# The order of a recurrence's score products on TensorE: head after head, or the two heads in turn

## The chip, the cores and the metric

The kernel runs on one core of one Trainium2 chip. The metric is the device time of one execution in microseconds (us). Before the change it is 2375.42 us, the median of three runs (2374.48 to 2377.20).

## The reference, cut to what matters

The program is a stack of blocks on one sequence of 512 positions and width 1024: an attention block with a gated feed-forward part, a block with an RWKV-7 recurrence and a feed-forward part, and a third block with two linear recurrences. Only the RWKV-7 block matters here. It runs a state recurrence for 16 heads of width 64, once forwards and once backwards in time:

```python
def rwkv7_scan(r, w, k, v, kk, a):
    def step(state, inp):
        r_t, w_t, k_t, v_t, kk_t, a_t = inp
        sa = jnp.einsum('bhvk,bhk->bhv', state, -kk_t)
        state = (state * w_t[:, :, None, :] + sa[..., None] * (kk_t * a_t)[:, :, None, :]
                 + v_t[..., None] * k_t[:, :, None, :])
        return state, jnp.einsum('bhvk,bhk->bhv', state, r_t)
```

For each direction the output is group-normed, a bonus term is added, and it is gated; the two directions are summed.

## The kernel before, in words

The recurrence is computed in chunks of 64 positions, eight chunks in each direction. The 16 heads are taken as eight pairs (`p` = 0 to 7); a pair fills the 128 partitions, head 0 the lower 64 (`H(0)`) and head 1 the upper 64 (`H(1)`). Chunk `n` of the forward direction goes with chunk `7 - n` of the backward one (`chunk_of`), and the two directions are worked on together (`d` = 0, 1).

Ten streams, written as Python generators, do the work of a pair. `front` (line 1483) and the two `half` (L1520, one for each direction) prepare the decayed keys and queries: the tiles `bk` (keys, one for each direction and each half of the chunks) and `ar` (queries). `scores` (L1602) multiplies them: in four blocks of two chunks (`i` = 0 to 3), for each head `hp` four matmuls of `bk` and `ar` that contract over that head's 64 partitions and write 128x128 results into an accumulator bank of PSUM. DVE then multiplies a head's bank with the causal masks `mk` into the tile `at` (the mask product), parts of `at` go by DMA to `nd_s` in DRAM, and PE transposes the `bk` of the block (L1636), which ACT copies into `at`. `inverse` (L1643) waits until the four blocks of a pair are done and inverts the 32x32 triangles, some sixty small DVE instructions on `X` and `xt_`, then stores `X`; `merge` (L1688) reads the inverses back through DMA as `yz` and joins them to 64x64; `mid` (L1737) forms the chunk's transition `m` from them (matmuls `ident,ar`, `uv,at`, `ax,tt`, `at,ta`); `chain` (L1798) carries the state `ss` through the eight chunks in a bank `cp` (matmuls `ss,m`; ACT writes the next `ss`); `post` (L1838) norms and gates the output `o`; `early` (L1666) prepares the values `uv`.

The order of all this is made while the program is built, by `weave` (L36). Each stream yields ahead of an operation the engine and the tiles that it needs, or a condition such as "the chain has done so many steps". `weave` keeps an own reckoning of when every engine will be free and every tile ready, and always advances the stream that could start first; the order in which instructions of one engine come out is then fixed. Its price for a matmul (`cost`, L48) lets two neighbours run side by side only where they differ in columns of the array; it makes no such allowance for rows, nor for the wait for an accumulator bank to come free.

All banks named `mb` come from one pool of five (`pm`), handed out in turn; `cp` has three of its own. A bank is written again once what was read from it five grants earlier has been read. The matmul helper is `MM` (L1302), so matmuls of all streams carry that line and are told apart by their tiles: the score products are `mb<-ar,bk`, 64 rows by 128 columns (`64*128`), each of them two instructions in the trace, since the operands are 32-bit floats. A run of one head in one block is thus eight instructions (x8), and the two heads on end sixteen (x16).

Of the kernel before, what the change touches and what calls it, by code (L numbers as in the profile page):

```python
# [24 lines left out]
class Net:  # L25
# [200 lines left out]
    def bank(self):  # L226
        return self.ps.tile([128, 512], F32, name="mm", tag="mm")
# [1063 lines left out]
    def rwkv(self, g_pre, mu_p, mu_n, w_r, w_k, w_v, w_o, k_k, k_a, r_k, gn_w, gn_b, w0, w1, w2, a0, a1, a2,  # L1291
# [5 lines left out]
        V, G = nc.vector, nc.gpsimd  # L1297
        TT = lambda e, o, a, b, op: e.tensor_tensor(out=o, in0=a, in1=b, op=op)  # L1298
# [3 lines left out]
        MM = lambda o, l, r, a, b: nc.tensor.matmul(o, lhsT=l, rhs=r, start=a, stop=b)  # L1302
        M, AD, SU, BY = ALU.mult, ALU.add, ALU.subtract, ALU.bypass
# [23 lines left out]
        with ExitStack() as c0:  # L1327
# [105 lines left out]
            with ExitStack() as c1:  # L1433
# [4 lines left out]
                mk = sh.tile([128, 2, 128], F32, name="mk")  # L1438
# [13 lines left out]
                bank = lambda: pm.tile([128, 512], F32, name="mb", tag="mb")  # L1452
                T2 = lambda tag, bufs=2: tp.tile([128, 520], F32, name="tmp", tag=tag, bufs=bufs)
                TQ = lambda: T2("tmq", 3)[:, :S]
                H = lambda i: slice(64 * i, 64 * i + 64)
# [3 lines left out]
                flat = lambda t: t.rearrange("p a b -> p (a b)")  # L1459
                chunk_of = lambda n: (n, 7 - n)  # L1460
                rows = lambda p: slice(p * 128, (p + 1) * 128)

                PE, AC, DV, PO = "PE", "Activation", "DVE", "Pool"
# [138 lines left out]
                def scores(p, st):  # L1602


                    nt_ = T2("nt", 1)[:, :S].rearrange("p (a b) -> p a b", b=32)
                    for i in range(4):
                        yield lambda: min(done["side", 0], done["side", 1]) > 2 * p + i // 2 and done["step"] >= 2 * (4 * p + i - 9) + 2
                        bk, ar = ([st[x] for x in y] for y in ((("bk", 0, i // 2), ("bk", 1, i // 2)), (("ar", 0), ("ar", 1))))
                        bks = lambda d, c: flat(bk[d][:, c % 4])

                        at = qp.tile([128, 2, 2, 3, 128], F32, name="at", tag="at")
                        for hp in range(2):
                            yield PE, *bk, *ar
                            b = bank().rearrange("p (j x) -> p j x", j=2)
                            for j in range(2):
                                for d in range(2):
                                    c = chunk_of(2 * i + j)[d]
                                    MM(b[:, j, 128 * d:128 * d + 128], bks(d, c)[H(hp)], flat(ar[d][H(hp), c]), True, True)
                            yield DV, b
                            TT(V, at[:, :, hp, 0::2, :], b.rearrange("p j (d x) -> p j d x", d=2), mk.unsqueeze(1).to_broadcast([128, 2, 2, 128]), M)  # L1620
                        yield DV, at
                        for g in (2, 3, 0, 1):
                            d = g // 2
                            e = 64 * d + 32 * (g % 2)
                            s_ = at[Q(g), :, :, 2 * d, e:e + 32].rearrange("p j h t -> p (j h) t")
                            if g >= 2:
                                V.transpose(out=nt_[Q(g), 4 * i:4 * i + 4], in_=s_)
                                s_ = nt_[Q(g), 4 * i:4 * i + 4]
                            nc.sync.dma_start(out=nd_d[p, 16 * g + 4 * i:16 * g + 4 * i + 4].rearrange("x (s t) -> s x t", t=32), in_=s_)
                        done["pre"] += i == 3  # L1630
                        st["at", i] = at
                        yield PE, *bk
                        b = bank().rearrange("p (j d x) -> p j d x", j=2, d=2)
                        for j in range(2):
                            for d in range(2):
                                nc.tensor.transpose(b[:, j, d, :], bks(d, chunk_of(2 * i + j)[d]), self.ident)  # L1636
                        done["bk"] += i % 2
                        yield AC, b
                        for j in range(2):
                            ACT(at[:, j, :, 1].rearrange("p h (d x) -> p h d x", d=2), b[:, j].rearrange("p d (h x) -> p h d x", h=2), AF.Copy)  # L1640
                        st["q", i] = at
# [247 lines left out]
                def each(f):  # L1889
                    for p in range(8):  # L1890
                        yield from f(p, sts[p])

                self.weave([(each(f), 0.0) for f in (
                    chain, mid, inverse, early, merge, scores, front, lambda p, st: half(p, st, 0), lambda p, st: half(p, st, 1), post)])


# [166 lines left out]
```

## Time and profile before

| | |
|---|---|
| median of three runs | 2375.42 us |
| the profiled execution | 2374.26 us, of which the span (first to last instruction) is 2372.5 us |
| TensorE matmul (PE) | busy 2148.4 us, 91% of the span |
| VectorE (DVE) | busy 1350.9 us, 57% |
| ScalarE (ACT) | busy 1084.0 us, 46% |
| GpSimd (POOL) | busy 82.7 us, 3% |
| mean granted TensorE clock | 0.936 of full speed |
| score products, whole program | 512 instructions, 85.4 us busy, 330 ns mean |

Most of the span is dense projections in other blocks. The recurrence lies between about 865 and 1390 us of the span: the score products run from 866.1 to 1284.7 us. A row of a timeline merges neighbouring instructions of one engine with the same line and tiles; its second number reaches from the first start to the last end, and the last end of a matmul lies beyond the start of the next row, because matmuls are pipelined. How long a run holds PE is therefore read from its start to the next row's start.

### The profile page before, as it was taken

The page shows a single profiled execution, that of the slowest core. Times are in us where ns is not written, and L with a number is a line of the kernel's source. Part 1 is how long each engine was busy: PE and PEld are TensorE (multiplying, and loading weights), DVE is VectorE, ACT ScalarE, POOL GpSimd, SP SyncE. Part 2 cuts the span into 40 slices and gives each one's busy share as a digit, 9 for nine tenths or more (in the row PEclk, how much of TensorE's full clock was granted, in tenths as well). Part 3 has the DMA queues.
Part 4 walks back from the last instruction along what each step waited for, and adds up shares of the span by engine and source line. Part 5 has one row for each costly group of instructions (what it writes and reads, how often), then busy time and mean ns, then how long its engine had stood idle before and what let it go on. Part 6 is the DMA issues. An engine that isn't in the chain of part 4 may idle for free. (4 is left out here: it accounts for less than half of the span.)

```text
span 2372.5 us, 36431 instructions
## 1 busy us (share of the span) xinstructions
PE 2148.4 (91%) x14218; PEld 1737.5 (73%) x14218; DVE 1350.9 (57%) x2862; ACT 1084.0 (46%) x1958; POOL 82.7 (3%) x121
## 2 busy tenths in 40 slices
PE   8998999999978965788888779999999999999998
PEld 6777788888756854667666658888787877788877
DVE  4556542333479568487867446287655657732353
ACT  4555353342356454567665645342333444532232
POOL 0000000000000001011111000000000000000000
PEclk9999999999979985788889989999999989899999
DMA  5311233233332423233323153234244454233341
GB/s 170 102 54 53 80 107 92 86 107 97 99 103 63 146 65 74 43 65 67 75 44 72 49 173 105 89 109 124 97 134 128 143 133 115 66 90 100 104 142 54
DMA packets 352375, 226.54 MB, mean 95 GB/s; under 512 B 114799, under 2 KB 306315, under 8 KB 352203
## 3 DMA queue, kind: packets, MB, share of 16 engines
q1 hardware_dynamic: 350762, 218.97, 32.8%
q10 hardware_dynamic: 1440, 5.24, 0.6%
q8 instruction: 112, 1.84, 0.3%
q14 instruction: 61, 0.49, 0.1%
HBM read 193.94 MB, written 27.07 MB: 93 GB/s over the span
## 5 line engine op out<-in xcount | busy, mean ns | idle before, releaser
L160 ACT ACTIVATE whi<-raw 128x1024 fp32r<-128x1024 f32 x228 | 239.6, 1052 | 603.0 <-PE mm L223 318.2
L161 DVE TENSOR_TENSOR wlo<-raw,whi 128x1024 fp32r<-128x1024 f32 x228 | 276.3, 1214 | 385.8 <-ACT whi L160 383.0
L222 PE MATMUL mm<-uth,whi 128*128 128x512 f32 (+1 forms) x1088 | 411.7, 380 | 1.7 <-ACT uth L196 1.7
L223 PE MATMUL mm<-utl,whi 128*128 128x512 f32 (+1 forms) x1088 | 406.0, 374 | 5.3 <-DVE utl L197 5.3
L224 PE MATMUL mm<-uth,wlo 128*128 128x512 f32 (+1 forms) x1088 | 406.2, 374 | 0.0
L223 PEld LDWEIGHTS mm<-utl,whi 128*128 128x128 f32 x1088 | 208.1, 191 | 42.9 <-DVE utl L197 6.6
L222 PEld LDWEIGHTS mm<-uth,whi 128*128 128x128 f32 x1088 | 207.8, 192 | 40.5 <-ACT uth L196 2.9
L224 PEld LDWEIGHTS mm<-uth,wlo 128*128 128x128 f32 x1088 | 208.0, 191 | 37.1 <-issue 1.1
L224 PE MATMUL mm<-whi,hl 128*128 128x512 f32 x512 | 200.6, 394 | 0.0
L222 PE MATMUL mm<-whi,hh 128*128 128x512 f32 x512 | 200.5, 394 | 0.0
L223 PE MATMUL mm<-wlo,hh 128*128 128x512 f32 x512 | 199.9, 393 | 0.0
L224 PEld LDWEIGHTS mm<-whi,hl 128*128 128x128 f32 x512 | 96.3, 188 | 22.0 <-issue 0.2
L223 PEld LDWEIGHTS mm<-wlo,hh 128*128 128x128 f32 x512 | 96.3, 188 | 21.7
L222 PEld LDWEIGHTS mm<-whi,hh 128*128 128x128 f32 x512 | 96.3, 188 | 21.4 <-issue 0.4
L1302 PE MATMUL mb<-ar,bk 64*128 64x128 f32 x512 | 85.4, 330 | 16.1 <-DVE ar L1298 13.8
L223 PE MATMUL mm<-mx,whi 128*128 128x512 f32 x224 | 91.3, 407 | 4.5 <-DVE mx L1289 4.4
L222 PE MATMUL mm<-whi,uth 128*128 128x512 f32 x224 | 88.5, 401 | 6.7 <-ACT whi L160 6.4
L222 PE MATMUL mm<-mx,whi 128*128 128x512 f32 x224 | 87.3, 410 | 7.2 <-ACT mx L1288 6.2
L1302 PEld LDWEIGHTS mb<-ar,bk 64*128 64x128 f32 x512 | 72.6, 227 | 24.6 <-issue 15.5
L224 PE MATMUL mm<-mx,wlo 128*128 128x512 f32 x224 | 90.0, 402 | 0.0
L224 PE MATMUL mm<-whi,utl 128*128 128x512 f32 x224 | 88.5, 398 | 0.0
L223 PE MATMUL mm<-wlo,uth 128*128 128x512 f32 x224 | 88.0, 396 | 0.0
(534 smaller groups left out, 3887.9 us busy)
## 6 DMA issues: line engine op xcount, KB each, us to landing
raw<-in_mlp_w_dram SPq DMA_DIRECT2D x128, 512.0 KB, 4.1
raw<-in_w_in_dram SPq DMA_DIRECT2D x44, 512.0 KB, 3.8
raw<-in_attn_w_in_dram SPq DMA_DIRECT2D x18, 512.0 KB, 4.2
gbt<-in_norm_g_dram ACTq DMA_DIRECT2D x8, 512.0 KB
raw<-in_attn_w_out_dram SPq DMA_DIRECT2D x8, 512.0 KB
raw<-in_rk_w_k_dram SPq DMA_DIRECT2D x8, 512.0 KB, 4.4
h_s<-h SPq DMA_DIRECT2D x8, 512.0 KB, 2.7
raw<-in_rk_w_v_dram SPq DMA_DIRECT2D x8, 512.0 KB
```

Source lines behind the costliest of these rows:

```text
L160: nc.scalar.activation(out=hi[:, :n], in_=raw[:, :n], func=AF.Copy)
L161: nc.vector.tensor_tensor(out=lo[:, :n], in0=raw[:, :n], in1=hi[:, :n].bitcast(F32), op=ALU.subtract)
L222: mm(out, lhsT=lhs[0], rhs=rhs[0], start=start, stop=False)
L223: mm(out, lhsT=lhs[0], rhs=rhs[1], start=False, stop=False)
L224: mm(out, lhsT=lhs[1], rhs=rhs[0], start=False, stop=stop)
L1302: MM = lambda o, l, r, a, b: nc.tensor.matmul(o, lhsT=l, rhs=r, start=a, stop=b)
```

## The change

In each block the score products of the two heads are now issued in turn, head 0, head 1, head 0, head 1, each head into a bank of its own, and both banks are taken before the first product. The two mask products follow after all eight matmuls. Before, each head's four matmuls were a step of their own, which `weave` could separate from the other head's by work of other streams.

```diff
                         at = qp.tile([128, 2, 2, 3, 128], F32, name="at", tag="at")
+                        yield PE, *bk, *ar
+
+                        bs = [bank().rearrange("p (j x) -> p j x", j=2) for _ in range(2)]
+                        for j in range(2):
+                            for d in range(2):
+                                c = chunk_of(2 * i + j)[d]
+                                for hp in range(2):
+                                    MM(bs[hp][:, j, 128 * d:128 * d + 128], bks(d, c)[H(hp)], flat(ar[d][H(hp), c]), True, True)
                         for hp in range(2):
-                            yield PE, *bk, *ar
-                            b = bank().rearrange("p (j x) -> p j x", j=2)
-                            for j in range(2):
-                                for d in range(2):
-                                    c = chunk_of(2 * i + j)[d]
-                                    MM(b[:, j, 128 * d:128 * d + 128], bks(d, c)[H(hp)], flat(ar[d][H(hp), c]), True, True)
-                            yield DV, b
-                            TT(V, at[:, :, hp, 0::2, :], b.rearrange("p j (d x) -> p j d x", d=2), mk.unsqueeze(1).to_broadcast([128, 2, 2, 128]), M)
+                            yield DV, bs[hp]
+                            TT(V, at[:, :, hp, 0::2, :], bs[hp].rearrange("p j (d x) -> p j d x", d=2), mk.unsqueeze(1).to_broadcast([128, 2, 2, 128]), M)
                         yield DV, at
```

As the streams yield elsewhere now, `weave` writes another order on every engine of the recurrence. Three places follow. First PE, at the third block (`i` = 2) of pair 3; `mb_` and a number is one grant of a bank, and the first number behind `bk` is the direction. Before:

```order
L1302 MATMUL mb_8410<-ar0_7911,bk01_7963 128x128
L1302 MATMUL mb_8410<-ar1_7915,bk11_7965 128x128
L1302 MATMUL mb_8410<-ar0_7911,bk01_7963 128x128
L1302 MATMUL mb_8410<-ar1_7915,bk11_7965 128x128
L1302 LDWEIGHTS zb_6290
L1302 MATMUL cp_8415<-zb_6290 128x256
L1302 MATMUL cp_8415<-uv0_7055,at_6920 64x64 x4
L1302 MATMUL cp_8415<-uv1_7056,at_6920 64x64 x4
L1302 MATMUL mb_8427<-ar0_7911,bk01_7963 128x128
L1302 MATMUL mb_8427<-ar1_7915,bk11_7965 128x128
L1302 MATMUL mb_8427<-ar0_7911,bk01_7963 128x128
L1302 MATMUL mb_8427<-ar1_7915,bk11_7965 128x128
```

The same place after the change:

```order
L1302 MATMUL mb_8407<-ar0_7908,bk01_7922 128x128
L1302 MATMUL mb_8408<-ar0_7908,bk01_7922 128x128
L1302 MATMUL mb_8407<-ar1_7916,bk11_7931 128x128
L1302 MATMUL mb_8408<-ar1_7916,bk11_7931 128x128
L1302 MATMUL mb_8407<-ar0_7908,bk01_7922 128x128
L1302 MATMUL mb_8408<-ar0_7908,bk01_7922 128x128
L1302 MATMUL mb_8407<-ar1_7916,bk11_7931 128x128
L1302 MATMUL mb_8408<-ar1_7916,bk11_7931 128x128
L1302 LDWEIGHTS zb_6290
L1302 MATMUL cp_8420<-zb_6290 128x256
```

Two runs of four matmuls, parted by work of the chain, have become one run of eight that changes banks at every matmul.

Second, DVE at the end of the inverse of pair 0; the `tmp` and `wl` rows prepare a later pair, `yz` is the inverse read back. Before:

```order
L1298 TENSOR_TENSOR xt__6800<-X,N 128x42
L1298 TENSOR_TENSOR tmp<-tmp,mb 128x512
L1298 TENSOR_TENSOR tmp<-tmp,k 128x512 x2
L1298 TENSOR_TENSOR X<-X,xt__6800 128x14x3
L1298 TENSOR_TENSOR tmp<-tmp 128x512 x2
L1298 TENSOR_TENSOR wl<-w,wh 128x512
L1298 TENSOR_TENSOR xt__6800<-X,N 128x30
L1298 TENSOR_TENSOR X<-X,xt__6800 128x15x2
L1298 TENSOR_TENSOR xt__6800<-X,N 128x15
L1298 TENSOR_TENSOR X<-X,xt__6800 128x15
L1662 MEMSET X 64x16 x2
L1700 STREAM_TRANSPOSE yz<-yz 128x512
```

After the change:

```order
L1298 TENSOR_TENSOR xt__6801<-X,N 128x30
L1298 TENSOR_TENSOR X<-X,xt__6801 128x15x2
L1298 TENSOR_TENSOR xt__6801<-X,N 128x15
L1298 TENSOR_TENSOR X<-X,xt__6801 128x15
L1664 MEMSET X 64x16 x2
L1298 TENSOR_TENSOR tmp<-tmp,mb 128x512
L1298 TENSOR_TENSOR tmp<-tmp,k 128x512 x2
L1298 TENSOR_TENSOR tmp<-tmp 128x512 x2
L1702 STREAM_TRANSPOSE yz<-yz 128x512
```

Five `tmp` rows have moved from ahead of the last `X` steps to behind them, and the `wl` row into the next pair's inverse.

Third, DVE at the end of the inverse of pair 4; `bk` and `ar` are those of pair 6. Before:

```order
L1298 TENSOR_TENSOR xt__9544<-X,N 128x15
L1298 TENSOR_TENSOR X<-X,xt__9544 128x15
L1662 MEMSET X 64x16 x2
L1298 TENSOR_TENSOR bk_10125<-tmp 128x4x64
L1298 TENSOR_TENSOR ar_10122<-tmp 128x4x64
```

After the change, from the sixth of the rows that went ahead:

```order
L1298 TENSOR_TENSOR ar_10114<-tmp 128x4x64
L1298 TENSOR_TENSOR bk_10124<-tmp 128x4x64
L1298 TENSOR_TENSOR ar_10110<-tmp 128x4x64
L1298 TENSOR_TENSOR bk_10124<-tmp 128x4x64
L1298 TENSOR_TENSOR ar_10110<-r,tmp 128x4x64
L1589 COPY wc<-tmp 64x8 x2
L1298 TENSOR_TENSOR tmp<-r,tmp 128x512
L1298 TENSOR_TENSOR bk_10115<-tmp 128x4x64
L1298 TENSOR_TENSOR ar_10114<-r,tmp 128x4x64
L1298 TENSOR_TENSOR X<-X,xt__9539 128x15
L1864 TENSOR_REDUCE rg<-tmp 128x8
L1664 MEMSET X 64x16 x2
```

Six `bk`, six `ar`, two `wc` instructions and one `tmp` stand now ahead of the last `X` step of that inverse, and one `rg` ahead of its last write. By the end of the next pair's inverse the two orders hold the same rows again.

## Rows read from the trace of the kernel before

**Rows 1.** Busy time by stage (us, instructions), PEclk: granted clock, DMA share, GB/s.
```profile
865.00:960.00 95.00, 55.27 (x618) 45.89 (x622) 76.00 (x212) 42.58 (x78) 9.12 (x13) 0.61 0.34 73
960.00:1290.00 330.00, 285.14 (x4112) 228.58 (x4104) 246.28 (x765) 224.00 (x578) 30.97 (x27) 0.86 0.27 56
1290.00:1390.00 100.00, 69.95 (x1090) 52.23 (x1090) 44.22 (x128) 57.86 (x160) 10.85 (x8) 0.88 0.35 92
```

**Rows 2.** Groups on PE, 865 to 960 us: xcount | busy, mean | idle before.
```profile
L1302 PE MATMUL mb<-ar,bk 64*128 64x128 f32 x144 | 25.5, 356 | 14.0 <-DVE ar L1298 13.8
```

**Rows 3.** Groups on PE, 960 to 1290 us, same columns.
```profile
L1302 PE MATMUL mb<-ar,bk 64*128 64x128 f32 x368 | 59.9, 320 | 2.1 <-DVE rg L1300 2.1
```

**Rows 4.** Timeline of PE: start, us, form, xcount [idle before <-releaser].
```profile
1042.64 2.07 PE L1302 MATMUL mb<-ar,bk 64*128 64x128 f32 x8
1044.64 1.22 PE L1302 MATMUL cp<-ss,m 128*128 128x128 f32 x4
...
1051.44 1.19 PE L1302 MATMUL mb<-at,ta 128*64 128x128 f32 x16
1052.56 1.16 PE L1302 MATMUL mb<-ar,bk 64*128 64x128 f32 x8
1053.65 0.28 PE L1302 MATMUL cp<-zb 128*128 128x256 bf16 x1
...
1058.10 1.71 PE L1302 MATMUL mb<-ar,bk 64*128 64x128 f32 x16
1059.74 0.28 PE L1302 MATMUL cp<-zb 128*128 128x256 bf16 x1
```

**Rows 5.** Waits of PE, 960 to 1290 us: total us, times, longest.
```profile
PE mb L1636 <- DVE at L1298: 1.2, 1, 1.2
```

**Rows 6.** Groups on DVE, 960 to 1290 us: the mask products.
```profile
L1298 DVE TENSOR_TENSOR at<-mb,mk 128x512 f32<-128x512 f32 x46 | 31.3, 688 | 32.4 <-PE mb L1302 31.9
```

**Rows 7.** Waits of DVE, 960 to 1290 us.
```profile
DVE at L1298 <- PE mb L1302: 31.9, 21, 6.4
DVE yz L1700 <- DMA yz<-xd_s: 13.9, 4, 5.1
DVE m L1298 <- PE mb L1302: 9.6, 7, 3.1
```

**Rows 8.** Waits of ACT, 960 to 1290 us.
```profile
ACT ss L1301 <- PE cp L1302: 28.0, 16, 3.4
ACT ta L1301 <- PE mb L1302: 21.1, 17, 3.0
ACT at L1301 <- PE mb L1636: 9.4, 5, 3.2
ACT tmp L1301 <- DVE rg L1862: 8.9, 4, 3.3
```

**Rows 9.** Timeline of DVE at the end of the inverse of pair 0.
```profile
941.32 0.69 DVE L1298 TENSOR_TENSOR tmp<-tmp,mb 128x512 f32<-128x512 f32 x1
...
943.13 0.20 DVE L1298 TENSOR_TENSOR X<-X,xt__6800 128x42 f32<-128x42 f32 x1
943.25 1.29 DVE L1298 TENSOR_TENSOR tmp<-tmp 128x512 f32<-128x512 f32 x2
...
945.05 0.18 DVE L1298 TENSOR_TENSOR xt__6800<-X,N 128x30 f32<-128x30 f32 x1
...
955.52 0.71 DVE L1700 STREAM_TRANSPOSE yz<-yz 128x512 f32<-128x512 f32 x1 [9.46 <-DMA yz<-xd_s]
```

**Rows 10.** Timeline of DVE after the inverse of pair 4.
```profile
1177.50 0.43 DVE L1298 TENSOR_TENSOR bk<-tmp 128x256 f32<-128x256 f32 x1
...
1183.21 0.42 DVE L1298 TENSOR_TENSOR bk<-tmp 128x256 f32<-128x256 f32 x1
...
1188.23 0.71 DVE L1700 STREAM_TRANSPOSE yz<-yz 128x512 f32<-128x512 f32 x1 [1.35 <-DMA yz<-xd_s]
```

**Rows 11.** Timeline of PE between the two runs of pair 6's first block.
```profile
1185.76 0.61 PE L1302 MATMUL mb<-selr,tmp 128*32 128x2 f32 x32 [1.31 <-DVE tmp L1298]
```

## The prediction

> **What bounds the kernel now.** I read the views from the coarse to the fine. Busy time by stage [rows 1] parts the recurrence in three. From 865 to 960 us DVE is the full engine (76.0 of 95 us) and PE is busy for 55.3: the first pairs are being prepared, and PE waits for the prepared `ar`, 13.8 us ahead of score products alone [rows 2]. From 960 to 1290 us PE is the fullest engine, 285.1 of 330 us, against 246.3 on DVE and 224.0 on ACT; this is the main stretch. From 1290 us on there are no score products left. So a saving on PE counts in the main stretch, and hardly ahead of it.
>
> What do the others wait for in the main stretch? The waits of DVE and of ACT [rows 7, 8] name PE most: of the seven longest, PE ended 31.9 + 9.6 + 28.0 + 21.1 + 9.4 = 100.0 us, the rest (a DMA, and DVE for ACT) 13.9 + 8.9 = 22.8. The longest of all, 31.9 us, is the mask product waiting for the score products. That is 81% for PE; the smaller waits lean to other causes, and I take 0.7 as the share of a PE saving that others would feel.
>
> **What the change removes on PE.** The timeline of PE shows the price of a score run [rows 4]. Eight instructions (one head of one block) hold PE from 1052.56 to 1053.65, 1.09 us, at the upper level of the granted clock (2.4 GHz); at the lower level (1.2 GHz) it is 1042.64 to 1044.64, 2.00 us. Where the two heads stood on end, sixteen instructions took 1058.10 to 1059.74, 1.64 us and not 2.18: the second head had already begun on its own 64 rows while the first still ran, which saved 2.18 - 1.64 = 0.54 us. So rows of the array do work side by side here, with two banks; only the order of issue limited it to a part of the run. What full alternation gives is shown by `at,ta`, which alternates between columns: sixteen instructions from 1051.44 to 1052.56, 1.12 us. I take 1.09 us for an alternating block, and 2.00 at the lower level.
>
> The main stretch has 368 score instructions [rows 3], which is 46 head runs in 23 blocks. In the timeline they are 36 runs of eight, 25 like the row at 1052.56 and 11 like the one at 1042.64, and 5 runs of sixteen (check: 25 x 1.16 + 11 x 2.07 + 5 x 1.71 = 60.3 us, against 59.9 us busy in [rows 3]). By blocks: 11 parted with both runs at the upper level save 11 x 1.09 = 12.0 us; 4 with both at the lower save 4 x 2.00 = 8.0; 3 mixed save the mean, 3 x 1.54 = 4.6; the 5 on end save 5 x (1.64 - 1.09) = 2.8. Together **27.4 us of PE time**. The 144 instructions ahead of 960 us [rows 2] would save some ten more, but there PE waits for DVE, so I cost that at nothing; if DVE stopped being the cover, it would come on top.
>
> Not all 27.4 us lie on the path. The first blocks of pairs 3 to 6 (at 1012, 1066, 1132 and 1182 us) come where PE waits for DVE's preparation, as between the two runs at 1182 and 1186 us [rows 11]: 3 x 1.54 + 2.00 = 6.6 us are taken off. Of the other 20.8 us, 0.7 reach the end: **-14.6 us**.
>
> **What it adds.** No instruction, no DMA, and nothing on POOL. A block takes two of five banks at once, so PE may stand at the second bank until its old content has been read, with all streams' matmuls queued behind. Nearest rows: PE's only wait in the main stretch on a mask product is 1.2 us, once [rows 5]; and reading a bank costs DVE 688 ns [rows 6]. Bounds: 0, and 23 x 0.69 = 15.9 us; a gain is excluded, as a wait on a bank cannot be negative. I take 0, being nearest to the 1.2 us, and keep the other end. The first mask product now follows eight matmuls and not four, but these eight take the time of the four, so it starts no later, and the second one starts earlier; what queues behind them on DVE, the steps of the inverse, moves up too. The DMA stores into `nd_s` keep their place behind the second mask product.
>
> Here stands a rule against the change. The two mask products of a block take 2 x 0.688 = 1.38 us of DVE [rows 6], more than the 1.09 us of the block on PE. The Trainium skill, "TensorEngine Tiling (Array Packing)", section Performance Considerations, says that tiling speeds up the matmuls and not the reading of PSUM, which may become the bottleneck. By that each block at the upper level shrinks to 1.38 us, an estimate: 11 x 0.80 + 8.0 + 3 x 1.40 + 5 x 0.26 = 22.3 us, and with the same 6.6 off and the same share 11.0 us, not 14.6. PE has other streams' work to put between blocks, so I stay with the sum by rows.
>
> **What it moves.** Two places of the new DVE order lie on the path. At the end of the inverse of pair 0, five `tmp` rows and `wl` went from ahead of its last steps to behind [rows 9]: they fill 941.32 to 943.13 and 943.25 to 945.05, 3.6 us, in the stretch that DVE bounds, and behind the inverse DVE sits idle for 9.46 us until the DMA brings `yz`, which hides them. The first chain starts that much sooner: **-3.6 us**. At the inverse of pair 4 it is the reverse: fourteen `bk`, `ar` and `wc`, a `tmp` and an `rg` went ahead of its end. Behind it they took 1177.50 to 1183.21, 5.7 us [rows 10], and the next `yz` waited only 1.35 us for its DMA, so little hides them. But pair 6 gets its operands as much sooner, for which PE waits there. I count half, **+2.9 us**.
>
> **Sum.** -14.6 - 3.6 + 2.9 = -15.3 us on the profiled execution's 2374.26 us (its span of 2372.5 and 1.8 around it). That execution lies 1.2 us under the median of 2375.42, so the median goes to **2360 us**.
>
> **The rivals.**
>
> B, all of it arrives. The whole 27.4 us and the 3.6 us: 2375.4 - 31.0 = 2344 us. For it: in the main stretch the granted clock is 0.86 of full [rows 1], a mixture of the two levels, and any run that came to lie at the upper one would add to it. Against: DVE would have 246 us to do in 303.
>
> C, the step of the chain takes its place. Between two steps of the chain PE now runs a score run while ACT writes the next `ss`; with half of them gone, PE stands and waits for ACT instead. What stays is the 5 runs on end, 2.8 x 0.7 = 2.0, and the moves, -3.6 + 5.7 in the bad case: 2375 us, no change. For it: chain steps and score runs do alternate in the order. Against: ACT waits for PE at `ss` 28.0 us, not PE for ACT [rows 8].
>
> D, slower: the DVE order decides. If the inverse of pair 4 ends 5.7 us late, its chain starts late by all of it; three `m` rows that moved ahead of pair 3's inverse add about 1 us; and if DVE gives the 3.6 us of the start back, since by the end of pair 1's inverse it has done the same rows, nothing is gained. With C's PE side that is 2375.4 + 6.7 = 2382 us. It decides when PE has nothing else to do while pair 4 is merged. Against: the waits of [rows 7], which put DVE behind PE.
>
> E, the change does less than it says: products pair only for a part of the run, as on end before, 1.64 us a block. Then 11 x 0.54 + 4 x 1.0 + 3 x 0.8 = 12.3 us of PE, less a quarter, times 0.7, and the moves: 2368 us. Against: alternating columns pair throughout [rows 4].
>
> **How the numbers follow.** About 0.2%, 4.75 us, is what a measurement of this kernel can tell from no change. Forecast 0.52 (2354 to 2367 us, with the share between 0.35 and 1), B 0.17, C 0.17, D 0.09, E 0.05. Forecast, B and E are faster: 0.74. C is the same: 0.17. D is slower: 0.09. The range from 2344 to 2375 us leaves out D, half of B and the upper edge of C, 0.2 in all; the bank bound of 15.9 us, set against the forecast, ends at 2376, on its edge.
>
> **What would show it.** Right: score rows of sixteen instructions with about 1.16 us, 32 of them; the group `mb<-ar,bk` at 45 to 55 us busy instead of 85.4; fewer DVE waits on it than 31.9 us; the last score product and the end of the recurrence 12 to 18 us earlier, and all that follows unchanged. Rows of 1.7 us would be E; new PE waits at `ss,m` on ACT would be C; PE waits on `at` products, the banks; a late `yz` of pair 4 with PE idle, D. A recurrence shortened by much more than 20 us, or not at all, makes the prediction wrong.

## The result, and the profile after

The change made the kernel faster: 2339.39 us, median of four runs (2335.87 to 2344.72), against 2374.95 us (2372.05 to 2377.20) for the kernel before in the same comparison. The ratio is 0.985, with an interval of 0.983 to 0.988. That is 35.6 us less where 15 were forecast; the median lies 4.6 us under the low end of the range. The profiled execution took 2337.59 us.

Busy time of the changed kernel by stage follows: first the stage ahead of the main stretch, then the main stretch as far as it now reaches, then everything from the first score product to the last product of the chain (columns as in [rows 1]).

```profile
865.00:960.00 95.00, 47.44 (x694) 38.64 (x696) 79.26 (x226) 44.77 (x83) 9.13 (x13) 0.64 0.33 72
960.00:1255.00 295.00, 248.81 (x4034) 197.32 (x4030) 244.56 (x757) 222.93 (x576) 33.28 (x29) 0.90 0.30 63
866.76:1338.00 471.24, 362.30 (x5792) 286.34 (x5792) 358.61 (x1090) 322.00 (x811) 48.20 (x44) 0.85 0.31 66
```

The last of these stretches, of the kernel before:

```profile
866.13:1374.00 507.87, 404.58 (x5792) 324.02 (x5792) 358.88 (x1090) 322.40 (x811) 47.71 (x44) 0.83 0.29 62
```

The two stretches hold the same 5792 matmuls. The stretch is 36.6 us shorter, which is the whole gain of the profiled execution (36.7 us); PE is busy for 42.3 us less, and idle for 5.6 us more (108.9 after, 103.3 before). I call it **the stretch** from here on, since it is the best yardstick of this study: three profiles of the changed kernel gave 471.2, 471.4 and 471.2 us. Its end is taken to the whole us, so it is good to about half a us.

The groups of score products on PE, ahead of 960 us and in the main stretch, answer to [rows 2, 3]:

```profile
L1302 PE MATMUL mb<-ar,bk 64*128 64x128 f32 x144 | 15.2, 359 | 16.5 <-DVE ar L1298 14.8 <-ACT at L1301 1.0 <-DVE tmp L1298 0.7
...
L1302 PE MATMUL mb<-ar,bk 64*128 64x128 f32 x368 | 31.6, 315 | 1.3 <-DVE ar L1298 0.8 <-ACT uv L1301 0.5
```

One instruction takes as long as before (315 ns against 320), but the group's busy time has almost halved, since products of both heads now run at a time: 59.9 to 31.6 us in the main stretch, 25.5 to 15.2 ahead of it. The timeline of PE shows a block at the upper level of the granted clock, among the steps of a chain (answers to [rows 4]):

```profile
1035.58 1.16 PE L1302 MATMUL mb<-ar,bk 64*128 64x128 f32 x16
1036.67 0.28 PE L1302 MATMUL cp<-zb 128*128 128x256 bf16 x1
...
1037.50 0.71 PE L1302 MATMUL cp<-ss,m 128*128 128x128 f32 x4
1038.05 0.27 PE L1302 MATMUL cp<-zb 128*128 128x256 bf16 x1
1038.25 0.69 PE L1302 MATMUL cp<-uv,at 128*64 128x64 f32 x16
1038.87 0.66 PE L1638 MATMUL mb<-ident,bk 128*128 128x128 f32 x4
1039.36 0.74 PE L1302 MATMUL cp<-ss,m 128*128 128x128 f32 x4
1040.03 1.16 PE L1302 MATMUL mb<-ar,bk 64*128 64x128 f32 x16
1041.12 0.28 PE L1302 MATMUL cp<-zb 128*128 128x256 bf16 x1
...
1041.95 0.73 PE L1302 MATMUL cp<-ss,m 128*128 128x128 f32 x4
```

Sixteen instructions hold PE from 1040.03 to 1041.12, 1.09 us, which is what eight took. No row here has an idle time in brackets: between these steps of the chain PE never stops. Over all eight chains it is idle for 16.4 of 179.7 us.

The waits of DVE, ACT and PE in the main stretch, for [rows 5, 7, 8]:

```profile
DVE at L1298 <- PE mb L1302: 9.6, 5, 3.1
DVE yz L1702 <- DMA yz<-xd_s: 9.1, 3, 5.1
DVE m L1298 <- PE mb L1302: 7.5, 4, 4.3
ACT ss L1301 <- PE cp L1302: 7.5, 8, 1.7
ACT ta L1301 <- PE mb L1302: 16.2, 14, 3.0
PE mb L1302 <- DVE at L1298: 1.6, 2, 1.4
PE cp L1302 <- ACT ss L1301: 1.0, 3, 0.7
```

Two waits have given way: DVE's mask product for the score products (31.9 to 9.6 us) and ACT's `ss` for the chain's products (28.0 to 7.5). PE's waits for banks and for `ss` are 1.6 and 1.0 us.

### The profile page after: what moved, and what is told of

Same layout as the page of the kernel before. It is cut to its first block, busy times and chain, and to the rows that moved or that the text cites. A ratio compares the mean times of both kernels' runs of the same rounds, so it can differ in the third digit from the quotient of the medians.

```text
span 2335.8 us, 36427 instructions
## 1 busy us (share of the span) xinstructions
PE 2105.7 (90%) x14218; PEld 1699.3 (73%) x14218; DVE 1350.6 (58%) x2862; ACT 1083.5 (46%) x1958; POOL 83.1 (4%) x121
## 5 line engine op out<-in xcount | busy, mean ns | idle before, releaser
L222 PE MATMUL mm<-uth,whi 128*128 128x512 f32 (+1 forms) x1088 | 412.1, 381 | 1.2 <-ACT uth L196 1.2
L282 DVE TENSOR_TENSOR acc<-mm,acc 128x512 f32<-128x512 f32 x48 | 33.0, 687 | 78.1 <-PE mm L224 78.1
L1301 ACT ACTIVATE ss<-cp,wc 64x64 f32<-64x64 f32 x224 | 69.1, 309 | 17.5 <-PE cp L1302 12.4
```

Source lines behind the costliest of these rows:

```text
L222: mm(out, lhsT=lhs[0], rhs=rhs[0], start=start, stop=False)
L282: nc.vector.tensor_tensor(out=a, in0=p, in1=a, op=ALU.add)
L1301: ACT = lambda o, i, f, **k: nc.scalar.activation(out=o, in_=i, func=f, **k)
```

## The experiments

The stretch parts into three: the **lead**, from the first score product to the first product of the chain (`cp<-ss,m`); the eight **chains**, each from the start of its pair's first such product to the end of its last; and the seven **gaps** between them. All are read from the trace of PE; lead, chains and gaps are rounded to the whole us after summing. The first yield of `scores` says which blocks run where: block `i` of pair `p` is released by step `2 * i` of the chain of pair `p - 2`. So the six **first** blocks (`i` = 0 of pairs 2 to 7) are released when that chain may begin, the eighteen **later** ones (`i` = 1 to 3) only in the midst of it, and the eight **early** ones (pairs 0 and 1) lie in the lead. So does the first block of pair 2, since there is no earlier chain to wait for.

Ratios go by the kernel before of the same comparison; e17 and e18 have a profile and no ratio, so that of their row is e13's and e11's. "Order" is that in which `weave` advances the streams: where an edit would have changed it, the recorded one of the kernel before (old) or of the changed kernel (new) was replayed. "Score" is the busy time of `mb<-ar,bk`; all times in us.

| label | order | paired blocks | ratio (interval) | stretch | lead / chains / gaps | PE busy, of it score |
|---|---|---|---|---|---|---|
| before | old | none (10 of 32 on end, 5 of them in the lead) | 1 | 507.9 | 106 / 204 / 198 | 404.6, 85.4 |
| after | new | all | 0.985 (0.983–0.988) | 471.2 | 102 / 180 / 190 | 362.3, 46.8 |
| e9, e15 | new | all | 0.986 (0.984–0.989), 0.984 (0.982–0.987) | 471.4, 471.2 | 102 / 180 / 190 | 362.7, 47.1 |
| e1 | old | all | 0.991 (0.989–0.994) | 488.4 | 105 / 184 / 199 | 372.1, 47.2 |
| e10 | old | all | 0.991 (0.989–0.993) | 491.4 | 105 / 182 / 204 | 371.4, 47.2 |
| e2 | new | all on end | 0.990 (0.988–0.992) | 479.6 | 104 / 190 / 185 | 386.3, 69.6 |
| e3 | new | none (a matmul between) | 0.996 (0.994–0.998) | 495.6 | 107 / 203 / 186 | 412.1, 89.4 |
| e11, e18 | new | none (keys between) | 1.000 (0.998–1.002) | 500.7, 500.7 | 105 / 206 / 189 | 413.2, 90.5 |
| e12 | new | all but the first | 0.990 (0.988–0.992) | 483.0 | 103 / 180 / 200 | 379.4, 57.3 |
| e5 | new | all but the first (a matmul between) | 0.990 (0.987–0.994) | 481.1 | 103 / 181 / 197 | 374.2, 57.6 |
| e14 | new | all but the early | 0.989 (0.987–0.991) | 478.0 | 106 / 182 / 190 | 379.3, 59.1 |
| e6 | new | all but the early (a matmul between) | 0.990 (0.988–0.993) | 481.1 | 107 / 182 / 192 | 382.5, 60.3 |
| e13, e17 | new | all but the later | 0.997 (0.996–0.999) | 499.0, 500.2 | 102 / 209 / 187 | 396.6, 70.7 |
| e16 | new | the later alone | 0.990 (0.988–0.992) | 482.1 | 106 / 178 / 199 | 387.0, 67.4 |
| e4 | row pairs priced half | all | 1.009 (1.007–1.012) | 528.1 | 106 / 187 / 235 | 374.2, 45.5 |
| e7 | the same, inverse leads | all | 0.995 (0.993–0.997) | 487.8 | 98 / 185 / 205 | 374.6, 47.3 |
| e8 | own price, inverse leads | all | 0.995 (0.992–0.997) | 490.0 | 97 / 196 / 198 | 372.1, 46.4 |

**Is it the pairing or the new order?** e1 keeps the order of before and pairs the products: at the first head's step both banks are taken and all eight matmuls issued in turn, and the second head's step issues nothing; each mask product reads its own bank of the two. e2 and e3 keep the new order and undo the pairing.

The edit of e1, against the kernel before:

```diff
 for hp in range(2):
     yield PE, *bk, *ar
-    b = bank().rearrange("p (j x) -> p j x", j=2)
-    for j in range(2):
-        for d in range(2):
-            c = chunk_of(2 * i + j)[d]
-            MM(b[:, j, 128 * d:128 * d + 128], bks(d, c)[H(hp)], flat(ar[d][H(hp), c]), True, True)
+    if hp == 0:
+        bs = [bank().rearrange("p (j x) -> p j x", j=2) for _ in range(2)]
+        for j in range(2):
+            for d in range(2):
+                c = chunk_of(2 * i + j)[d]
+                for h in range(2):
+                    MM(bs[h][:, j, 128 * d:128 * d + 128], bks(d, c)[H(h)], flat(ar[d][H(h), c]), True, True)
```

The edit of e3, against the changed kernel; e2 is the same without the `if hp:` and the line on `zb`:

```diff
-for j in range(2):
-    for d in range(2):
-        c = chunk_of(2 * i + j)[d]
-        for hp in range(2):
+for hp in range(2):
+    if hp:
+        MM(bs[1][:, :, 0:128], zb, zb.unsqueeze(1).to_broadcast([128, 2, 128]), True, True)
+    for j in range(2):
+        for d in range(2):
+            c = chunk_of(2 * i + j)[d]
             MM(bs[hp][:, j, 128 * d:128 * d + 128], bks(d, c)[H(hp)], flat(ar[d][H(hp), c]), True, True)
```

What the small matmul writes is written over by the second head's products.

> The order of before is kept on DVE, ACT and POOL, step by step; on PE alone the second head's four score products move up to the first head's, and the two heads alternate. So this is the pairing of rows without a new order. Theory P (on PE, what the score runs lose in the main stretch comes off the end whole): the score group falls from 85.4 to about 47 us busy, and the time by about 28 us, to 2347 us (ratio 0.988). Theory O (the larger part came from the new order, and only a share of the PE time counts, as the prediction had it): about 15 us, 2360 us (0.994).

> The order of the changed kernel is kept on DVE, ACT and POOL; inside each block the four products of head 0 stand ahead of the four of head 1, so the rows pair only where one run ends and the next begins. A block should take about 1.64 us at the upper clock instead of 1.09. Theory P: 23 blocks of the main stretch times 0.55 us, a quarter more for runs at the lower clock, some 16 us more than the changed kernel: 2355 us (0.992). Theory O: the order is that of the changed kernel, so most of the gain stays: 2345 us (0.987).

> As the run before, and a small matmul over all 128 rows of the array stands between the two heads, whose result is overwritten and unused, so that no rows pair at all; order of the changed kernel otherwise. A block should take about 2.4 us at the upper clock (1.09, 0.22, 1.09). Theory P: some 35 us more than the changed kernel, back to about 2375 us (1.000). Theory O: the new order is worth its part even so: 2355 us (0.992).

e1 gained 0.9%, and e3 0.4% without any pairing, so both parts count. The thirds of the stretch tell them apart. In the old order pairing shortened the chains, 204 to 184, and left the lead at 105 (106 before) and the gaps at 199. The new order without pairing (e3) left the chains at 203 and shortened the gaps, 198 to 186. In the old order pairing takes 19.5 us off the stretch (16.5 in e10, the same kernel again), and the new order another 17.2 (20.2) once the products are paired; by medians the second part is smaller, 12 us (2352.08 in e10, 2340.18 in e9 beside it). e2 shows that to stand the heads on end in one step is most of the way: 8.4 us short of full alternation.

**Does the order slow it, if `weave` is told the truth?** e4 gives the reckoning the price that the hardware showed:

```diff
...
-                (_, col), (rows, m) = i.tile_position, i.tile_size
+                (row, col), (rows, m) = i.tile_position, i.tile_size
+                pair = rows == 64 and m == 128 and rows_[0] not in (None, row)
+                rows_[0] = row if rows == 64 and m == 128 else None
...
-                c = passes * (max(n, 64) if one or i.is_transpose else m / 2 if beside else max(n, m)) * 0.417e-3
+                c = passes * (max(n, 64) if one or i.is_transpose else m / 2 if beside or pair else max(n, m)) * 0.417e-3
```

> The changed kernel, but the planner's price for a matmul lets neighbours on different rows run side by side, so it plans with about half the time for score products and makes another order on all engines. Theory P: PE's work is the same, so the time stays within some 8 us of the changed kernel's 2339 us, to either side, by what the order does. Theory O (the order is worth as much as the pairing): a truer price gives a further gain of 10 us or more, about 2328 us (0.980).

The right price gave the worst order, which neither theory had: 57 us more than the changed kernel with the same products paired, 45 of it in the gaps. The waits of e4 from 960 us to its last chain say where:

```profile
PE mb L1304 <- ACT yz L1303: 53.1, 15, 16.5
ACT yz L1303 <- DVE yz L1704: 50.8, 6, 13.2
```

ACT and PE wait for DVE's `yz`, the inverse read back, up to 13.2 us at a time; in the changed kernel this wait of ACT is 15.8 us in all. The likely cause was that `weave` had put other streams' rows on DVE ahead of the inverse. e7 is e4 with a lead of 0.1 for the inverse's stream in `weave`'s choice, e8 the changed kernel with that lead and the old price:

```diff
-self.weave([(each(f), 0.0) for f in (
+self.weave([(each(f), {2: 0.1}.get(n, 0.0)) for n, f in enumerate((
     chain, mid, inverse, early, merge, scores, front, lambda p, st: half(p, st, 0), lambda p, st: half(p, st, 1), post))])
```

> The planner with the truer price of the run before, which was 22 us slower than the kernel before; in addition the inverse's steps win ties on DVE by a lead of 0.1 us. In its order the other streams' DVE rows inside the inverses of pairs 2 and 4 fall from 48 and 46 us to about 27 each. If the long inverses made that order slow (stretches of 66 and 63 us, with 55 and 56 us between the chains around them): the time falls by some 40 us to about 2355 us or less (0.992). If something else in that order is slow: it stays above 2380 us.

> The changed kernel with its own price and the inverse's lead of 0.1 us: the other streams' DVE rows inside the inverse of pair 4 fall from 30 to 21 us. If the time between two chains is set by the inverse behind others on DVE: some 5 to 10 us less than the changed kernel, 2332 us (0.982). If the order is a lottery whose parts cannot be told: within 15 us to either side.

e7 takes the wait of ACT for `yz` from 50.8 to 2.5 us, and 40 us of the stretch with it, so the starved inverse was most of e4's loss. Both kernels have the shortest lead of all (98 and 97), and lose it again in gaps and chains; neither beats the changed kernel. Both expectations of e8 fell: it was to be within 15 us of the changed kernel at the worst, and its stretch is 19 us longer.

**Which blocks count?** e5 and e6 part the heads of the first and of the early blocks with the small matmul of e3.

> The changed kernel in its own order; only in the first block of pairs 2 to 7 a small matmul (result overwritten, unused) parts the two heads, so these six blocks do not pair. That is the term of the prediction that took the first blocks off the path. If it is right (PE waits for DVE there, between one chain and the next): the time stays within 4 us of the changed kernel's 2339 us (ratio about 0.985). If first blocks lie on the path as others do: six blocks at 1.3 to 2.5 us each, some 12 us more, 2351 us (0.990).

> The same, but in the four blocks each of pairs 0 and 1, ahead of 960 us, where the prediction costed the saving at nothing because DVE bounds the stretch. If right: within 4 us of 2339 us (0.985). If the gain ahead of 960 us counted: eight blocks at 1.3 to 2.5 us, some 15 us more, 2354 us (0.991).

Either loses ten us of the stretch. A lower clock does not explain it in e5, whose granted clock in the stretch is 0.85 as in the changed kernel. The kernels from e11 on add no work: a block that isn't to pair has its own four key transposes, which otherwise follow the block, between its heads.

Here is e12; in the place of `i == 0 and p > 1`, e11 has `True`, e13 and e17 `i > 0 and p > 1`, e14 `p < 2`, and e16 `i == 0 or p < 2`.

```diff
+keys = None
+for hp in range(2) if i == 0 and p > 1 else ():
+    if hp:
+        keys = bank().rearrange("p (j d x) -> p j d x", j=2, d=2)
+        for j in range(2):
+            for d in range(2):
+                nc.tensor.transpose(keys[:, j, d, :], bks(d, chunk_of(2 * i + j)[d]), self.ident)
+    for j in range(2):
+        for d in range(2):
+            c = chunk_of(2 * i + j)[d]
+            MM(bs[hp][:, j, 128 * d:128 * d + 128], bks(d, c)[H(hp)], flat(ar[d][H(hp), c]), True, True)
+if not (i == 0 and p > 1):
+    for j in range(2):
...
```

> The changed kernel once more, as the measure for the three runs beside it: 2339 us, ratio 0.983 to 0.988 as before. Nothing is told apart by it alone.

> The first run once more, beside the changed kernel: the order of before, rows paired. If the pairing gives about half the gain and the new order the rest, as the first four runs suggest: 0.989 to 0.994, some 15 us slower than the changed kernel. If that difference was the spread between runs: within 5 us of the changed kernel.

> The new order with no pairing and no work added: in every block the four transposes of the keys (which PE does for the block anyway) stand between the two heads' products. If the new order is worth some 15 us by itself: 2358 us (0.993). If pairing is all: 2375 us (1.000). Chain stretches should sum to about 204 us, as before and as in the kernel with the added matmul, and the times between chains to 185 to 190 us.

> The same only in the first blocks of pairs 2 to 7, so that these six do not pair; no work added. If first blocks lie off the path: within 4 us of the changed kernel beside it. If they count as others do: some 8 us slower (0.5 to 1.1 us at the upper clock, twice that at the lower).

e9 and e10 repeat what they repeat. With nothing paired the new order is not measurably faster than the kernel before (e11), but its stretch is 7 us shorter. e11 has a price of its own, though. The timeline of PE in e11:

```profile
1048.92 0.71 PE L1306 MATMUL cp<-ss,m 128*128 128x128 f32 x4
...
1050.37 0.49 PE L1306 MATMUL cp<-ss,m 128*128 128x128 f32 x2
1051.04 0.49 PE L1306 MATMUL cp<-ss,m 128*128 128x128 f32 x2 [0.18 <-ACT ss L1305]
1051.45 1.16 PE L1306 MATMUL mb<-ar,bk 64*128 64x128 f32 x8
1052.54 0.66 PE L1625 MATMUL mb<-ident,bk 128*128 128x128 f32 x4
1053.13 1.16 PE L1306 MATMUL mb<-ar,bk 64*128 64x128 f32 x8
...
1055.04 0.71 PE L1306 MATMUL cp<-ss,m 128*128 128x128 f32 x4
```

Two steps of the chain with a block between go from 1048.92 to 1055.04, where the next one starts: 6.12 us. The changed kernel takes 4.45 us for the same instructions (1037.50 to 1041.95). Of the 1.67 us between them, 1.08 are the unpaired products; 0.41 is the second step (1050.37 to 1051.45, 1.08 us against 0.67), in which PE now waits for `ss`, since the keys that stood ahead of it are gone; the rest, 0.18, lies on other rows. e3, whose keys stay in their place, has the cleaner order and an added matmul instead (0.2 us a block, some 7 us in all). The same two steps in e3:

```profile
1051.71 0.71 PE L1306 MATMUL cp<-ss,m 128*128 128x128 f32 x4
...
1053.57 0.74 PE L1306 MATMUL cp<-ss,m 128*128 128x128 f32 x4
1054.25 1.16 PE L1306 MATMUL mb<-ar,bk 64*128 64x128 f32 x8
1055.33 0.28 PE L1306 MATMUL mb<-zb 128*128 128x256 bf16 x1
1055.55 1.16 PE L1306 MATMUL mb<-ar,bk 64*128 64x128 f32 x8
...
1057.46 0.71 PE L1306 MATMUL cp<-ss,m 128*128 128x128 f32 x4
```

They take 5.75 us, 1.30 more than in the changed kernel: 0.22 for the added matmul and 1.08 for the unpaired products. So a block unpaired between two steps costs its PE time, and the 0.41 us belong to e11's way of parting the heads; for eighteen later blocks that would be some 7 us, an estimate from this one place. So the new order alone is worth 7 us by e11 and 12 by e3; e11's price and e3's added work make it rather more than less.

> The order of the changed kernel, with every block paired but the eighteen later blocks (i = 1 to 3) of pairs 2 to 7, between whose heads the block's four key transposes stand. No work is added. Measured so far: all blocks unpaired in this way 1.0 of before, the six first blocks unpaired 0.990, none unpaired 0.986. Theory W (TensorE time arrives whole, wherever it is saved): the eighteen blocks cost some 43.4 - 10.2 - 13.5 = 20 us of TensorE time (90.5 us of score products with all unpaired less 47.1 with none; 57.3 - 47.1 for the first blocks; 60.3 - 46.8 for the early ones), so 20 us over the changed kernel: 2360 us, 0.9945. Theory S (what arrives depends on the place: the first blocks count in full since DVE and ACT are held up behind them, the later ones in part): the three parts must add up to the 33 us between all and none, 12 of which the first blocks and some 11 the early ones have taken, so 10 us: 2350 us, 0.990.

> The same for the eight blocks of pairs 0 and 1 alone, whose products lie ahead of about 960 us. No work is added (the earlier run on these blocks parted the heads with a small matmul more). The prediction's step (ahead of 960 us TensorE waits for DVE, so what is saved there costs nothing): no change from the changed kernel, 2340 us, 0.986. Theory W: the whole 13 us of TensorE time, 2353 us, 0.9915. Theory S leaves it open, at 11 us by the earlier run: 2351 us, 0.9905.

> The changed kernel again, as the mark for the other two of this call. All theories: 0.986 of before, 2340 us.

Both theories on e13 fell: without the later blocks 28 us are lost, of 29.5 for all blocks, so the losses of the three groups add up to 46. (Some 7 of the 28 may be the price of the moved keys.)

> The order of the changed kernel, with only the eighteen later blocks (i = 1 to 3 of pairs 2 to 7) paired; the first blocks of these pairs and all blocks of pairs 0 and 1 have the four key transposes between their heads. The stretch from the first score product to the end of the last chain is 471.2 us with all paired (three profiles within 0.2 us), 500.7 with none, 483.0 without the six first ones, 478.0 without the eight early ones, 499.0 without the eighteen later ones. Theory L (the later blocks, which stand between two steps of the chain, are what arrives; the others help only as far as the chain is short): the losses of the first and the early blocks add up, 471.2 + 11.8 + 6.8 = 490 us, 0.9925 of before, and the later blocks alone are worth 11 us, though without them the others are worth 2. Theory M (the later blocks alone bring nearly all, and first and early ones cover for one another): 480 to 484 us, 0.989. Theory N (any part missing spoils the whole): 497 us or more, 0.998.

> A second profile of the kernel without the pairing of the eighteen later blocks. Its first one fell on the longest of its runs. If the 499.0 us of the stretch from the first score product to the end of the last chain belong to the kernel, they come again within 2 us, with ACT's waits for the chain's products at 35 us or more; if they belong to that run, the stretch is nearer to 490 us.

> A second profile of the kernel with no block paired in the new order. All theories: 500.7 us for the stretch from the first score product to the end of the last chain, within 2 us, so that the new order without pairing is 7 us shorter there than the kernel before (507.9).

e17 and e18 repeat the stretches within 1.2 us. e16 gave 482.1 us: the later blocks alone bring 18.6 of the 29.5 us, and theory M holds. The waits of ACT for the chain's products, from 960 us to the last chain, go with the later blocks among the kernels with keys between the heads. First e11 (none paired), then e17 (all but the later), then e16 (the later alone), then the changed kernel, and last e3 (none paired, keys in their place):

```profile
ACT ss L1305 <- PE cp L1306: 34.6, 18, 4.6
```

```profile
ACT ss L1305 <- PE cp L1306: 38.3, 20, 4.6
```

```profile
ACT ss L1305 <- PE cp L1306: 12.3, 10, 4.6
```

```profile
ACT ss L1301 <- PE cp L1302: 12.4, 10, 4.6
```

```profile
ACT ss L1305 <- PE cp L1306: 23.1, 16, 4.6
```

So about half of e11's surplus over the changed kernel goes with the moved keys and not with the missing pairs. The chains are 206 and 210 us in e11 and e17, 178 and 180 in e16 and the changed kernel, and 203 in e3. No version beat the changed kernel. A lead for the inverse of pair 0 alone, which e7 and e8 suggest, was not tried.

## Why the prediction was wrong

The mechanism on PE was right: rows of sixteen with 1.16 us, a PE saving of 28.3 us in the main stretch (59.9 less 31.6) where 27.4 were worked out. What failed is how much of the PE time reaches the end, and the worth of the moves. The gain of the stretch can be parted in two ways, by the runs: the order first (before, e11, e16, after), or the pairing first (before, e1, after; e10 in brackets).

| step of the prediction | forecast | shown, order first | shown, pairing first |
|---|---|---|---|
| 20.8 us of PE time, share 0.7 | -14.6 | -18.6 (the later blocks alone) | -19.5 (-16.5), all blocks |
| first blocks and those ahead of 960 us, at nothing | 0 | -10.9 | in the row above |
| moves, -3.6 + 2.9 | -0.7 | -7.2 (-12 by e3) | -17.2 (-20.2) |
| sum | -15.3 | -36.7 | -36.7 |

The first way gives the pairing too much and the order too little, since e11 pays some 7 us for its moved keys, by the estimate above. The second has no such price, though e1 ran at a lower granted clock than the changed kernel (see 5), and by it the term on PE was near (2 to 5 us short) and the moves were the miss, of 16 to 20 us. By either way the moves are worth ten times what was priced, or more, and what the pairing brings depends on the order, which a sum of terms read from the old order can't show.

1. **"I cost that at nothing", of the blocks ahead of 960 us, and "6.6 us are taken off", of the first blocks.** In the old order this holds: e1 and e10 pair these blocks too, and their lead is 105 us and their gaps are 199 and 204, against 106 and 198 before. In the new order it fails, by 11 us. Where the early blocks pair there, the lead is 102 or 103 us (after, e5, e12, e13); where they don't, it is 105 to 107 (e3, e6, e11, e14, e16). I took PE's wait of 13.8 us for `ar` [rows 2] as cover for what follows it, and most of it was cover: in the lead PE is busy for 71.7 us in e11 and 54.8 in the changed kernel, and of these 16.9 us only 3.6 come off. The first blocks act mostly on the gaps: 200 us without their pairing (e12), 190 with. A wait of PE shows that PE was early there, not that the time of the next matmuls is free.

2. **The share of 0.7.** It was an average over places that differ, the very thing that the stages are to keep apart. Between the chain's steps the PE time comes off whole: 1.08 us for an unpaired block in e3, and in the old order 20 us of the chains (204 to 184 in e1), in which the score products are busy for 43.8 us before and 23.7 in e1. In the gaps and the lead of the old order it brings nothing. In the new order the later blocks save 23.1 us of score time (90.5 less 67.4) and shorten the chains by 28 and the stretch by 18.6, since the gaps grow by 9 (189 to 199). The gaps are back at 190 when the first blocks pair too (e14). So the groups need each other: with the chains long, the pairing of the others brings 1 us (500.7 to 499.0 or 500.2); with the chains short, 11. Why is argued, not shown: long chains leave the other streams time to prepare the next pair, and short ones put that preparation on the path.

3. **The moves.** This is the step that failed by either way: -0.7 us was forecast, -7 to -12 came without the pairing and -17 to -20 with it. The inverse of pair 0 without the `tmp` rows [rows 9] was to start the first chain 3.6 us sooner. In the changed kernel it does, by just that (105.5 to 101.9 us), but not by the moves alone: e11 has the order without the pairing and its lead is 105 us, e1 has the pairing without the order and its lead is 105 too. Only both together shorten it, so the right number is in part luck. The gap behind the chain of pair 3, where pair 4 is merged, was to grow by 2.9 us [rows 10]; it is 38 us before and 37 after. Most of the order's gain without pairing lies in the gap behind the chain of pair 2 (31 us before, 23 in e11, 24 after). Which rows of the new order bring it, no run shows.

4. **Banks at nothing.** Right: PE waits for a mask product to free a bank 1.6 us in the main stretch, against 1.2 before. The Trainium skill, "TensorEngine Tiling (Array Packing)", section Performance Considerations, says that copying from PSUM may become the bottleneck after TensorE is sped up, with four times as its example. The trace shows no sign of it at two times: a block holds PE for 1.09 us and not the 1.38 of my estimate, and DVE still waits for PE at the mask products (9.6 us) more than PE for DVE (1.6). The 23 blocks stand in 295 us, which may be why.

5. **The granted clock** was left out of the sum but for rival B. In the main stretch it went from 0.86 to 0.90. The 5280 matmuls that are not score products are busy 315.5 us in the stretch (362.3 less 46.8), 3.7 less than before, and 322.7 in e11. So some of the saving comes as a clock that is granted for other matmuls, and that is not the same in every order. Between the two orders with paired products it is more: 324.9 us in e1 at a granted clock of 0.81 in the stretch, against 0.85 in the changed kernel. These 9.4 us of PE time are more than half of the 17.2 that part the two; how many of them arrive, and what in the new order raises the clock, stays open.

**The rivals.** B's 2344 us is the nearest number: as much came as the main stretch's whole PE time and more. But not by its sum: part of it comes from the order, and the 3.6 us of the lead came only with the pairing. C is refuted: PE's wait for `ss` is 1.0 us. The point I held against it, that ACT waits for PE at `ss` [rows 8], was a row to build on: this wait fell by 20.5 us. D did not come, but is real: e4, with the same products, is 0.9% slower than before, although its products pair: its order takes more than all that the pairing brings. E is refuted by the rows of 1.16 us. What the prediction itself named as its failure, "a recurrence shortened by much more than 20 us", is what came.

## What to carry to other kernels

Ask of each saving where it stands, not what share of the engine's time is waited for: between the steps of a serial chain the fullest engine's time came off whole here, while behind a wait for another engine it was worth nothing in one order and 11 us in another. When a list scheduler writes the order, a change of a step's size moves things everywhere; replay the old order to separate the change from its order, and expect the order alone to be worth as much as the change (here 7 to 12 us gained by the new order without the pairing and 17 to 20 with it, and 57 lost by a third order with the same products). A truer price made the order worse: the scheduler looks only at which stream could start first, and not at which one the next chain waits for.

## What the runs showed of the hardware

Most of the spread of the runs lies outside the changed part. After the last chain, the same matmuls take 994 to 1008 us, and the granted clock goes along. The windows from the last chain to the end, of the third run of the changed kernel (e15), then of e5:

```profile
1337.00:2331.04 994.04, 948.73 (x4485) 773.17 (x4484) 547.78 (x1083) 367.03 (x500) 17.67 (x42) 0.97 0.38 112
```

```profile
1352.00:2360.06 1008.06, 961.52 (x4484) 783.29 (x4484) 547.56 (x1083) 366.55 (x499) 17.65 (x42) 0.96 0.38 111
```

PE is busy 12.8 us longer for the same work, DVE and ACT are not. The stretch itself repeated within half a us (changed kernel), 1.2 us (e13 and e17) and 3.0 us (e1 and e10). So here a window around the changed work told apart what the medians didn't: e11 is 7 us shorter than before by its stretch, in both of its profiles (of the kernel before there is one), where the runs show no difference.

Two halves of the array's rows pair fully, at both levels of the clock: sixteen instructions in the time of eight, 1.16 us at the upper and 2.08 at the lower, as in this row of the changed kernel's timeline (granted clock 0.50 of full speed):

```profile
1050.57 2.08 PE L1302 MATMUL mb<-ar,bk 64*128 64x128 f32 x16
```

On end they pair for about half: 69.6 us for all blocks (e2), between 47 paired and 90 apart.
